# Gates without GpSimd and staging on both sides of SBUF, in an encoder layer with product-key experts

## The chip, the cores and the metric

The kernel runs on one core of one Trainium2 chip. The core has a matrix engine (PE), a vector engine (VectorE, DVE in the profile), a scalar engine (ScalarE, ACT), GpSimd (POOL), the sync engine's queue (SP) for transfers, and 16 DMA engines. Its on-chip memories are SBUF, with 128 partitions, and PSUM, where matrix products are summed. The metric is device time in microseconds for one execution. Before the change the median of three runs is 3086.2 us (3084.46 to 3092.26).

## The reference

One layer of an encoder over 1024 tokens of width 1024: a projection, differential attention and retention, an output projection added to x, and then PEER, a feed-forward layer made of 16384 single-neuron experts, of which each token uses 8 x 16. The change lies in PEER:

```python
q = (xb @ w_query).reshape(tb, PEER_HEADS, 2, PEER_KEY_DIM // 2)
s = jnp.einsum('thpd,hpnd->thpn', q, sub_keys)
top_s, top_i = lax.top_k(s, PEER_TOPK)                   # 16 of 128 rows, 16 of 128 columns
cand_s = top_s[:, :, 0, :, None] + top_s[:, :, 1, None, :]
cand_i = top_i[:, :, 0, :, None] * N_KEYS + top_i[:, :, 1, None, :]
best_s, pos = lax.top_k(cand_s, PEER_TOPK)               # the best 16 of the sums
eid = take_along_axis(cand_i, pos)
gate = softmax(best_s)
act = gelu(einsum('thkd,td->thk', expert_down[eid], xb))
out = einsum('thk,thkd->td', gate * act, expert_up[eid])
```

An expert is a pair (row, column) of a grid of 128 x 128.

## The kernel before

The eight blocks of 128 tokens are worked on in two ways after the output projection. Five of them (set B) compute PEER densely: the activations of all 16384 experts, times a gate that is zero for nearly all, times all expert values. The other three (set A) fetch the rows of their chosen experts one by one with indirect transfers that POOL issues (line 988) and that DVE reduces (lines 998 and 1007). Products in full precision are three products of parts: an operand is split by ACT into a high part (`uh`, `hh`, `vh`, `wqh`) and by DVE or POOL into the rest (`ul`, `hl`, `vl`, `wql`).

Four stretches follow one another:

- **The choice of experts** (648 to 899 us in the profile), for set B and one block of set A, so n = 6 blocks at once. For each of 8 heads and both key sets, PE computes queries (`pq`) and scores (`psc`), and DVE takes the best 16 (lines 723 to 728). Then `choose` finds where the winners came from: DVE compares positions with a ramp (line 778, `eq`, 6 x 16 x 16 elements in bf16), first for rows and then for columns, and POOL multiplies the result by the indices `tif` (line 779); sums over it give the expert's row and column. `sel` (line 788) takes the gate. POOL also makes `wql` (line 656), `pql` (636) and, for five blocks of experts whose dense activations are computed ahead here, `ul` (858).
- **The gates** (899 to 1124 us). For each of 5 blocks (i) the choices are transposed (`gtp`, copied to `kT` and `gT`). Then for each group of 4 tokens, 32 groups per block: DVE compares a ramp with the tokens' rows and columns at once (line 920, `oh`, bf16); ACT copies one half into `bo` in f32 (924); the other half is multiplied by the gate into `ao`, by POOL (927) in 29 groups of 32 and by ACT (930) in 3; PE multiplies the two for each token (933), which puts the gates of one token on the grid of experts in PSUM (`pg`, six buffers); and DVE (936, 13 groups of 32) or ACT (938, 19 of 32) copies them into `stg`, 64 KB per partition. When a block is done, eight transfers of 1 MB store `stg` to `g_dr` in DRAM (940), in runs of 512 bytes. `oh`, `bo` and `ao` have four buffers each, `stg` two, both in one pool.
- **The start of the dense stage** (1124 to 1222 us). Five blocks of expert weights, `first0` to `first4` (512 KB each), are loaded, split, and multiplied (`products`, `pa`, gelu into `hfirst`); beside each of them four of set A's fetched rows are reduced with `xng`. Then their gates are read back from `g_dr` into the same tiles, multiplied by `hfirst` (1070) and split again, and the product with the expert values begins (`up`, tiles `po`). `acc` holds the sums, begun with x.
- **The dense stage** (1222 us to the end): for the other blocks of experts the same, with the rest of the fetching beside it.

Instructions of one engine run in order. The program writes the work stage by stage; a scheduler orders each engine's queue by need, so operations of neighbouring steps mix. A tile pool on the left or right side of SBUF gives its room back when it closes, and what is placed there later waits until the last reader of the old tiles is done. The tiles of the fetched rows (`rows`, `xng`, `gacc`) and the `first` tiles lie on the right side.

## Time and profile before

| | us |
|---|---|
| median of three runs | 3086.2 |
| profiled execution, its own time | 3082.46 |
| its span, first to last instruction | 3080.7 |
| PE busy in the span | 2830.5 (92%) |
| DVE busy | 2556.9 (83%) |
| POOL busy | 1678.9 (54%) |
| ACT busy | 1055.1 (34%) |

The rows further down come from the trace of the profiled execution. A row of a timeline gives the start, the time, the engine, the line of the program, the operation and the tiles (out<-in), and in brackets the idle time before it with what ended it; equal operations in a row are one entry with a count. A row of a table by stretches gives, for PE, weight loads, DVE, ACT and POOL in this order, busy microseconds and the number of instructions, then the granted clock of PE as a share of full speed, the DMA engines' busy share and the rate in GB/s. Busy time includes time in which an operation has begun and stands still.

### The profile page before, as it was taken

The page shows a single profiled execution, that of the slowest core. Times are in us where ns is not written, and L with a number is a line of the kernel's source. Part 1 is how long each engine was busy: PE and PEld are TensorE (multiplying, and loading weights), DVE is VectorE, ACT ScalarE, POOL GpSimd, SP SyncE. Part 2 cuts the span into 40 slices and gives each one's busy share as a digit, 9 for nine tenths or more (in the row PEclk, how much of TensorE's full clock was granted, in tenths as well). Part 3 has the DMA queues.
Part 4 walks back from the last instruction along what each step waited for, and adds up shares of the span by engine and source line. Part 5 has one row for each costly group of instructions (what it writes and reads, how often), then busy time and mean ns, then how long its engine had stood idle before and what let it go on. Part 6 is the DMA issues. An engine that isn't in the chain of part 4 may idle for free.

```text
span 3080.7 us, 44740 instructions
## 1 busy us (share of the span) xinstructions
PE 2830.5 (92%) x15999; PEld 2512.8 (82%) x15999; DVE 2556.9 (83%) x4867; ACT 1055.1 (34%) x1734; POOL 1678.9 (54%) x1335
## 2 busy tenths in 40 slices
PE   8999798898978846999999999999999999999998
PEld 6887577698976646988888888898999889989997
DVE  6466587579999955899999998988999889889997
ACT  4444566422237742222322222222222222222222
POOL 3422455245659954566656556566554466565551
PEclk9999999999999977999999999999999999999999
DMA  4334865353205688998898888999999899999994
GB/s 166 108 118 142 194 123 110 133 195 129 104 18 138 190 224 318 326 324 319 302 323 292 305 328 332 328 331 322 338 324 326 295 355 327 327 333 332 331 323 157
DMA packets 334832, 770.87 MB, mean 250 GB/s; under 512 B 26640, under 2 KB 133776, under 8 KB 334608
## 3 DMA queue, kind: packets, MB, share of 16 engines
q0 software_dynamic: 128128, 438.36, 41.2%
q1 hardware_dynamic: 203888, 324.72, 31.8%
q10 hardware_dynamic: 2592, 4.93, 0.5%
q8 instruction: 126, 2.06, 0.3%
q14 instruction: 98, 0.80, 0.1%
HBM read 678.70 MB, written 89.19 MB: 249 GB/s over the span
## 4 chain that ended last, share of the span: by engine, by line
PE 19%; issue 17%; DVE 16%; POOL 10%; DMA 7%; ACT 2%; SPq 1%; POOLq 0%; DVEq 0%; ACTq 0%
POOL rows L988 8%; DVE rows L998 3%; PE po L73 3%; PE po L75 3%; DVE gacc L1007 3%; PE po L74 3%; PE pa L73 3%; PE pa L74 3%; PE pa L75 3%; DVE oh L920 2%; DMA ur<-ut 2%; DMA rows<-peer_u,idx 1%; DVE acc L1104 1%; DMA vr<-peer_v 1%; POOL ao L927 1%
## 5 line engine op out<-in xcount | busy, mean ns | idle before, releaser
L988 POOL DMA_INDIRECT rows<-peer_u,idx x384 | 525.8, 1369 | 411.3 <-DVE act L998 248.0
L73 PE MATMUL pa<-nThB,uh 128*128 128x320 f32 x2048 | 636.4, 311 | 54.7 <-ACT uh L1060 39.8
L988 POOL DMA_INDIRECT rows<-peer_v,idx x384 | 469.6, 1223 | 393.8 <-DVE gacc L1007 326.5
L75 PE MATMUL pa<-nThB,ul 128*128 128x320 f32 x2048 | 633.8, 310 | 14.1 <-DVE ul L1061 14.1
L74 PE MATMUL pa<-nTlB,uh 128*128 128x320 f32 x2048 | 634.3, 310 | 0.0
L73 PE MATMUL po<-vh,hh 128*128 128x512 f32 x1280 | 511.0, 400 | 46.0 <-DVE acc L1104 40.8
L75 PE MATMUL po<-vh,hl 128*128 128x512 f32 x1280 | 505.2, 395 | 0.0
L74 PE MATMUL po<-vl,hh 128*128 128x512 f32 x1280 | 504.3, 394 | 0.0
L1007 DVE SCALAR_TENSOR_TENSOR gacc<-rows,act,gacc 128x1024 f32<-128x1024 f32 x384 | 493.3, 1285 | 6.2 <-DMA rows<-peer_v,idx 5.3
L998 DVE CUSTOM_DVE_ANT_0 rows<-rows,xng 128x1024 f32<-128x1024 f32 x384 | 459.3, 1226 | 34.9 <-DMA rows<-peer_u,idx 20.5
L73 PEld LDWEIGHTS pa<-nThB,uh 128*128 128x128 f32 x2048 | 387.7, 189 | 61.0 <-ACT uh L1060 40.0
L75 PEld LDWEIGHTS pa<-nThB,ul 128*128 128x128 f32 x2048 | 387.8, 189 | 15.8 <-DVE ul L1061 15.4
L74 PEld LDWEIGHTS pa<-nTlB,uh 128*128 128x128 f32 x2048 | 387.6, 189 | 4.4
L73 PEld LDWEIGHTS po<-vh,hh 128*128 128x128 f32 x1280 | 244.0, 191 | 103.6 <-DVE acc L1104 49.6
L1092 ACT ACTIVATE vh<-vr 128x512 fp32r<-128x512 f32 x256 | 160.5, 628 | 414.4 <-DMA vr<-peer_v 197.2
L75 PEld LDWEIGHTS po<-vh,hl 128*128 128x128 f32 x1280 | 243.8, 190 | 54.8 <-DVE hl L1077 0.4
L74 PEld LDWEIGHTS po<-vl,hh 128*128 128x128 f32 x1280 | 244.1, 191 | 46.6
L1060 ACT ACTIVATE uh<-ur 128x1024 fp32r<-128x1024 f32 x118 | 125.2, 1061 | 360.5 <-PE pa L74 226.6
L1061 DVE TENSOR_TENSOR ul<-ur,uh 128x1024 fp32r<-128x1024 f32 x118 | 144.3, 1223 | 106.3 <-ACT uh L1060 104.6
L933 PE MATMUL pg<-ao,bo 128*128 128x128 f32 x1280 | 182.2, 290 | 40.3 <-POOL ao L927 31.7
L927 POOL TENSOR_TENSOR ao<-oh,gT 128x512 f32<-128x512 bf16 x145 | 206.9, 1461 | 22.0 <-DVE oh L920 22.0
L868 ACT ACTIVATE hf<-pa 128x320 f32<-128x320 f32 x246 | 105.7, 430 | 328.9 <-PE pa L75 319.0
(346 smaller groups left out, 5415.0 us busy)
## 6 DMA issues: line engine op xcount, KB each, us to landing
vr<-peer_v SPq DMA_DIRECT2D x256, 256.0 KB, 6.0
ur<-ut SPq DMA_DIRECT2D x123, 512.0 KB, 5.7
g_dr<-stg SPq DMA_DIRECT2D x40, 1024.0 KB, 10.1
gt<-g_dr SPq DMA_DIRECT2D x123, 320.0 KB, 4.9
wr<-w_in SPq DMA_DIRECT2D x48, 512.0 KB, 3.8
wqr<-wq SPq DMA_DIRECT2D x16, 576.0 KB, 5.3
wq_dr<-wqh SPq DMA_DIRECT2D x16, 576.0 KB, 4.7
wq_dr<-wql SPq DMA_DIRECT2D x16, 576.0 KB, 3.3
```

Of the source, the lines that this page charges most:

```text
L73: PE.matmul(out, ah, bh, start=first, stop=False)
L74: PE.matmul(out, ah, bl, start=False, stop=False)
L75: PE.matmul(out, al, bh, start=False, stop=last)
L868: S.activation(hf[:, cs], pa, AF.Gelu)
L927: G.tensor_tensor(ao, oh[0], bc(gT[:, q:q + 4, None], [P, 4, P]), op=ALU.mult)
L933: PE.matmul(pg[:, j], bo[:, j], ao[:, j], start=True, stop=True)
L988: G.indirect_dma_start(out=u, out_offset=None, in_=table, in_offset=bass.IndirectOffsetOnAxis(ap=idx, axis=0))
L998: V.tensor_tensor_reduce(out=u, in0=u, in1=xn, scale=1.0, scalar=0.0, op0=ALU.mult, op1=ALU.add, accum_out=act[:, k:k + 1])
L1007: V.scalar_tensor_tensor(o, v, act[:, k:k + 1], o, op0=ALU.mult, op1=ALU.add)
L1060: S.activation(uh, ur, AF.Copy)
L1061: V.tensor_tensor(ul, ur, uh.bitcast(F32), op=ALU.subtract)
L1092: S.activation(vh, vr, AF.Copy)
```

## The change

POOL's operations in the choice are issued in pieces: `wql` in three of 384 elements, the multiplication `eq` in three of 512, `ul` in two of 512. In the gates `ao` is always made by DVE and `stg` always copied by ACT. `stg` has one buffer on the left side of SBUF (blocks 0, 2, 4) and one on the right (blocks 1, 3). Once the stores of block 3 are written into the program, the right one is closed, and the tiles of fetched rows and the `first` tiles are placed there; the `first` loads go from ACT's queue, after the gates, to SP's, ahead of the last block's stores.

```diff
@@ -653,7 +653,9 @@
             wh = pool.tile([P, 9, P], F32R, name="wqh")
             wl = pool.tile([P, 9, P], F32R, name="wql")
             S.activation(wh, wr, AF.Copy)
-            G.tensor_tensor(wl, wr, wh.bitcast(F32), op=ALU.subtract)
+
+            for b in range(0, 9, 3):
+                G.tensor_tensor(wl[:, b:b + 3], wr[:, b:b + 3], wh[:, b:b + 3].bitcast(F32), op=ALU.subtract)
             for k, w in enumerate((wh, wl)):
                 nc.sync.dma_start(wq_dr[hp, k], w.bitcast(F32))
             return wh, wl
@@ -776,7 +778,10 @@
                 for a, pl in ((0, row), (1, col)):
                     eq = pw.tile(sh, BF16, name="eq")
                     V.tensor_tensor(eq, bc(pl[:, :, None, :], sh), bc(iot[:, None, :, :], sh), op=ALU.is_equal)
-                    (V if last and not a else G).tensor_tensor(eq, eq, bc(tif[:, :, a, :, None], sh), op=ALU.mult)
+                    en = V if last and not a else G
+                    for b in [(0, n)] if n < 4 else [(b, b + 2) for b in range(0, n, 2)]:
+                        o = eq[:, b[0]:b[1]]
+                        en.tensor_tensor(o, o, bc(tif[:, b[0]:b[1], a, :, None], [P, b[1] - b[0], TOPK, TOPK]), op=ALU.mult)
                     if wb > 1:
                         eqs.append((a, eq))
                     else:
@@ -855,7 +860,9 @@
             for b, e, ur in rooms:
                 (queue or nc.sync).dma_start(ur, ap["ut"][a][:, b:e])
                 S.activation(uh[:, b:e], ur, AF.Copy)
-                (en or V).tensor_tensor(ul[:, b:e], ur, uh[:, b:e].bitcast(F32), op=ALU.subtract)
+                for c in range(b, e, 4):
+                    (en or V).tensor_tensor(ul[:, c:c + 4], ur[:, c - b:c - b + 4], uh[:, c:c + 4].bitcast(F32),
+                                            op=ALU.subtract)
             return uh, ul
 
         def products(ps, hf, bufs, uh, ul):
@@ -899,10 +906,14 @@
 
 
         g_dr = dram.tile([P, P, wB], F32, name="g_dr")
+        pros = ExitStack()
         with ExitStack() as es:
             pc = es.enter_context(tc.tile_pool(name="gc", bufs=1))
             pw = es.enter_context(tc.tile_pool(name="gw", bufs=4))
-            pg_ = es.enter_context(tc.tile_pool(name="gs", bufs=2))
+
+            odd = ExitStack()
+            pgs = [es.enter_context(tc.tile_pool(name="gs0", bufs=1)),
+                   odd.enter_context(tc.tile_pool(name="gs1", bufs=1, side="right"))]
             ps = es.enter_context(tc.tile_pool(name="gps", bufs=2, space=PSUM))
             iop = pc.tile([P, P, 4], BF16, name="iop")
             G.iota(iop, pattern=[[1, P], [0, 4]], base=0, channel_multiplier=0, allow_small_or_imprecise_dtypes=True)
@@ -914,7 +925,7 @@
                 V.tensor_copy(kT, pT[:, 0:2])
                 gT = pw.tile([P, P], F32, name="gT", bufs=1)
                 V.tensor_copy(gT, pT[:, 2])
-                stg = pg_.tile([P, P, P], F32, name="stg")
+                stg = pgs[i % 2].tile([P, P, P], F32, name="stg")
                 for q in range(0, P, 4):
                     o2 = pw.tile([P, 2, P, 4], BF16, name="oh")
                     V.tensor_tensor(o2, bc(iop[:, None], [P, 2, P, 4]), bc(kT[:, :, None, q:q + 4], [P, 2, P, 4]),
@@ -923,25 +934,24 @@
                     bo = pw.tile([P, 4, P], F32, name="bo")
                     S.activation(bo, oh[1], AF.Copy)
                     ao = pw.tile([P, 4, P], F32, name="ao")
-                    if q // 4 % 11:
-                        G.tensor_tensor(ao, oh[0], bc(gT[:, q:q + 4, None], [P, 4, P]), op=ALU.mult)
-                    else:
-                        for j in range(4):
-                            S.activation(ao[:, j], oh[0][:, j], AF.Copy, scale=gT[:, q + j:q + j + 1])
+                    V.tensor_tensor(ao, oh[0], bc(gT[:, q:q + 4, None], [P, 4, P]), op=ALU.mult)
                     pg = ps.tile([P, 4, P], F32, name="pg", bufs=6)
...
                     dst, src = stg[:, :, q:q + 4], pg.rearrange("p t a -> p a t")
-                    if q // 4 % 5 in (0, 2):
-                        V.tensor_copy(dst, src)
-                    else:
-                        S.activation(dst, src, AF.Copy)
+                    S.activation(dst, src, AF.Copy)
                 for k in range(0, P, 16):
                     nc.sync.dma_start(g_dr.rearrange("a b t -> b a t")[:, k:k + 16, i * P:(i + 1) * P], stg[:, k:k + 16])
+                if i == (nB - 2 if nB % 2 else nB - 1):
+                    odd.close()
+                    gp = top.enter_context(tc.tile_pool(name="gp", bufs=1, side="right"))
+                    pp = pros.enter_context(tc.tile_pool(name="pro", bufs=1, side="right"))
+                    firsts = [pp.tile([P, DC * P], F32, name=f"first{a}") for a in range(FIRST)]
+                    for a, ur in enumerate(firsts):
+                        nc.sync.dma_start(ur.rearrange("p (c e) -> p c e", e=P), ap["ut"][a])
         early.close()
 
 
-        gp = top.enter_context(tc.tile_pool(name="gp", bufs=1, side="right"))
         late = {}
 
         def tail(t, o):
@@ -1119,30 +1129,27 @@
...
-            with tc.tile_pool(name="pro", bufs=1, side="right") as pp:
-                first = [pp.tile([P, DC * P], F32, name=f"first{a}") for a in range(FIRST)]
-                for a, ur in enumerate(first):
-                    S.dma_start(ur.rearrange("p (c e) -> p c e", e=P), ap["ut"][a])
-                load(FIRST)
...
+            load(FIRST)
+            for a, ur in enumerate(firsts):
+                raw[a] = ur.rearrange("p (c e) -> p c e", e=P)
...
+            for a in range(FIRST):
+                down(a)
+            pros.close()
```

**DVE, the beginning of the gates.** Before, `oh` is the comparison and `stg<-pg` the copy of a group out of PSUM:

```order
L914 CAST kT<-gtp 128x256
L916 COPY gT<-gtp 128x128
L920 TENSOR_TENSOR oh<-iop,kT 128x1024 x5
L936 COPY stg<-pg 128x128x4
L920 TENSOR_TENSOR oh<-iop,kT 128x1024 x2
L936 COPY stg<-pg 128x128x4
L920 TENSOR_TENSOR oh<-iop,kT 128x1024 x4
L936 COPY stg<-pg 128x128x4
```

and in the changed program, `ao<-oh,gT` is the multiplication by the gate:

```order
L925 CAST kT<-gtp 128x256
L927 COPY gT<-gtp 128x128
L931 TENSOR_TENSOR oh<-iop,kT 128x1024 x2
L937 TENSOR_TENSOR ao<-oh,gT 128x512 x2
L931 TENSOR_TENSOR oh<-iop,kT 128x1024 x2
L937 TENSOR_TENSOR ao<-oh,gT 128x512 x2
L931 TENSOR_TENSOR oh<-iop,kT 128x1024 x2
L937 TENSOR_TENSOR ao<-oh,gT 128x512 x2
```

The copies are gone from DVE, and each pair of comparisons is followed by its two multiplications.

**SP, the end of the gates.** `g_dr<-stg` are the stores of a block (32 for the first four), `x_dr` the residual x in DRAM, `gt` and the later `first` loads the gates read back. Before:

```order
L940 DMA g_dr<-stg 128x16x128 x32
L1044 DMA ur<-ut 128x1024
L940 DMA g_dr<-stg 128x16x128 x8
L1089 DMA vr<-peer_v 128x512 x2
L1143 DMA acc_10860<-x_dr_70 128x1024
L1143 DMA acc_10861<-x_dr_71 128x1024
L1143 DMA acc_10862<-x_dr_72 128x1024
L1143 DMA acc_10863<-x_dr_73 128x1024
L1143 DMA acc_10864<-x_dr_74 128x1024
L1053 DMA gt<-g_dr 128x640
L1004 DMA gacc<-x_dr_75 128x1024
L1141 DMA first_10868<-g_dr 128x640
```

and in the changed program:

```order
L944 DMA g_dr<-stg 128x16x128 x32
L951 DMA first_10471<-ut 128x1024
L951 DMA first_10472<-ut 128x1024
L951 DMA first_10473<-ut 128x1024
L951 DMA first_10474<-ut 128x1024
L951 DMA first_10475<-ut 128x1024
L1014 DMA gacc<-x_dr_75 128x1024
L1054 DMA ur<-ut 128x1024
L944 DMA g_dr<-stg 128x16x128 x8
L1099 DMA vr<-peer_v 128x512 x2
L1147 DMA first_10471<-g_dr 128x640
L1147 DMA first_10472<-g_dr 128x640
```

The five loads of weights stand between the fourth and the fifth block's stores, and the `acc` loads have gone behind the gates of the five blocks.

**ACT, the fifth block of the gates.** `xng` is the input that the first fetched rows are reduced with. Before:

```order
L924 ACTIVATE bo<-oh 128x512 x3
L938 ACTIVATE stg<-pg 128x128x4 x3
L1125 DMA first_10868<-ut 128x1024
L1125 DMA first_10869<-ut 128x1024
L1125 DMA first_10870<-ut 128x1024
L1125 DMA first_10871<-ut 128x1024
L1125 DMA first_10872<-ut 128x1024
L1060 ACTIVATE uh<-first_10868 128x1024
L994 DMA xng<-xn_dr_83 128x1024
L1060 ACTIVATE uh<-first_10869 128x1024
```

and in the changed program:

```order
L935 ACTIVATE bo<-oh 128x512
L942 ACTIVATE stg<-pg 128x128x4
L935 ACTIVATE bo<-oh 128x512
L1004 DMA xng<-xn_dr_83 128x1024
L942 ACTIVATE stg<-pg 128x128x4 x2
L935 ACTIVATE bo<-oh 128x512 x4
L942 ACTIVATE stg<-pg 128x128x4 x2
L935 ACTIVATE bo<-oh 128x512
L942 ACTIVATE stg<-pg 128x128x4
L935 ACTIVATE bo<-oh 128x512
```

The weight loads have left this queue; `bo` and `stg` alternate; and the load of `xng`, which stood behind all gates, stands ahead of the last eight `bo`.

## Rows read from the trace of the kernel before

**Rows 1.** Busy time by stage: stretch, length, busy us per engine, clock, DMA, GB/s:
```profile
648.50:899.00 250.50, 222.10 (x1549) 218.38 (x1547) 239.71 (x1327) 56.94 (x100) 143.68 (x93) 0.93 0.30 106
899.00:1124.10 225.10, 183.64 (x1292) 158.29 (x1290) 219.00 (x235) 167.29 (x315) 206.94 (x145) 0.98 0.55 152
1124.10:1222.00 97.90, 40.88 (x241) 39.89 (x241) 34.11 (x52) 11.78 (x20) 33.44 (x25) 0.71 0.96 324
1222.00:3080.70 1858.70, 1792.42 (x10000) 1620.36 (x10000) 1664.19 (x2654) 498.12 (x798) 1034.24 (x827) 0.99 0.89 316
```

**Rows 2.** One line's instructions (least/median/longest ns): the comparison of columns:
```profile
L778 DVE TENSOR_TENSOR eq<-col,iot x8: 951/3424/3426, 675.1 to 889.1; 128x1536 bf16<-128x1536 bf16 x8
```

**Rows 3.** Timelines of POOL and DVE in one head (start us, us):
```profile
828.85 2.78 POOL L779 TENSOR_TENSOR eq<-eq,tif 128x1536 bf16<-128x1536 bf16 x1 [6.13 <-DVE eq L778]
...
829.02 3.42 DVE L778 TENSOR_TENSOR eq<-col,iot 128x1536 bf16<-128x1536 bf16 x1
```

**Rows 4.** Timeline of DVE: small operations caught beside POOL:
```profile
672.56 2.46 DVE L765 TENSOR_TENSOR col<-tc__6080,ex 128x96 bf16<-128x96 f32 x1
...
678.60 2.84 DVE L788 TENSOR_TENSOR sel<-be,gsm 128x96 f32<-128x96 f32 x1
...
867.44 2.43 DVE L788 TENSOR_TENSOR sel<-be,gsm 128x96 f32<-128x96 f32 x1
```

**Rows 5.** One line's instructions: line 779 later, in pieces of 512:
```profile
L779 POOL TENSOR_TENSOR eq<-eq,tif x6: 1042/1060/2154, 1358.5 to 1483.5; 128x512 bf16<-128x512 bf16 x6
```

**Rows 6.** Busy time in three heads of the choice:
```profile
671.70:705.50 33.80, 33.05 (x258) 32.73 (x258) 31.84 (x156) 8.84 (x16) 25.14 (x16) 1.00 0.41 137
...
733.90:762.30 28.40, 25.11 (x176) 24.79 (x175) 28.26 (x166) 5.88 (x11) 18.10 (x12) 0.88 0.37 125
...
762.30:797.40 35.10, 32.16 (x231) 32.02 (x231) 30.80 (x165) 10.39 (x16) 20.68 (x13) 0.95 0.35 126
```

**Rows 7.** Timeline of DVE: the first instruction of the gates:
```profile
899.01 0.42 DVE L914 CAST kT<-gtp 128x256 bf16<-128x256 f32 x1 [3.07 <-PE gtp L912]
```

**Rows 8.** Timelines of DVE, POOL, ACT and PE in the gates:
```profile
944.37 1.88 DVE L920 TENSOR_TENSOR oh<-iop,kT 128x1024 bf16<-128x1024 bf16 x3
...
945.82 14.45 POOL L927 TENSOR_TENSOR ao<-oh,gT 128x512 f32<-128x512 bf16 x10 [1.70 <-DVE oh L920]
...
947.82 2.38 ACT L924 ACTIVATE bo<-oh 128x512 f32<-128x512 bf16 x4
...
948.63 4.12 PE L933 MATMUL pg<-ao,bo 128*128 128x128 f32 x32 [0.33 <-POOL ao L927]
...
953.03 1.16 PE L933 MATMUL pg<-ao,bo 128*128 128x128 f32 x8 [0.29 <-POOL ao L927]
```

**Rows 9.** One line's instructions: POOL's `ao`, and line 779 on DVE:
```profile
L927 POOL TENSOR_TENSOR ao<-oh,gT x145: 1032/1492/1512, 900.9 to 1121.2; 128x512 f32<-128x512 bf16 x145
...
L779 DVE TENSOR_TENSOR eq<-eq,tif x1: 1752/1752/1752, 887.4 to 887.4; 128x1536 bf16<-128x1536 bf16 x1
```

**Rows 10.** Timeline of DVE: a subtraction of 512 elements:
```profile
1213.38 0.69 DVE L1093 TENSOR_TENSOR vl<-vr,vh 128x512 fp32r<-128x512 f32 x1
```

**Rows 11.** Timelines of ACT, PE and POOL after the gates:
```profile
1123.53 0.60 ACT L938 ACTIVATE stg<-pg 128x512 f32<-128x512 f32 x1 [1.41 <-PE pg L933]
...
1163.26 0.64 PE L73 MATMUL pa<-nThB,uh 128*128 128x320 f32 x1 [39.77 <-ACT uh L1060]
...
1221.99 0.79 PE L73 MATMUL po<-vh,hh 128*128 128x512 f32 x1 [5.13 <-ACT hh L1076]
...
1160.27 0.94 POOL L988 DMA_INDIRECT rows<-peer_u,idx  x1 [0.30 <-issue]
...
1184.97 1.99 POOL L988 DMA_INDIRECT rows<-peer_u,idx  x1 [0.30 <-issue]
```

**Rows 12.** Chain of waits: the last stores landing (start us, us, what):
```profile
1145.49 10.85 DMA g_dr<-stg
```

**Rows 13.** Busy time in ten microseconds of loads without stores:
```profile
1160.00:1170.00 10.00, 6.74 (x30) 6.51 (x31) 2.45 (x2) 3.52 (x5) 4.11 (x4) 0.60 1.02 409
```

More of the change, by code (lines that the diff above doesn't have):

```diff
@@ L1119, in up @@
                         add(k, t)
-            with tc.tile_pool(name="pro", bufs=1, side="right") as pp:
-                first = [pp.tile([P, DC * P], F32, name=f"first{a}") for a in range(FIRST)]
-                for a, ur in enumerate(first):
-                    S.dma_start(ur.rearrange("p (c e) -> p c e", e=P), ap["ut"][a])
-                load(FIRST)
-                for a, ur in enumerate(first):
-                    raw[a] = ur.rearrange("p (c e) -> p c e", e=P)
-                    split_u(a)
-                    ready[a] = ready[a], pp.tile([P, wB], F32, name=f"hfirst{a}")
-                    products(ps, ready[a][1], 2, *ready[a][0])
-                    ready[a] = ready[a][1]
-                    for _ in range(4):
-                        next(gen)
-                split_u(FIRST)
-                load(FIRST + 1)
-                values(0)
-                values(1)
-                for a, ur in enumerate(first):
-                    gts[a] = ur[:, 0:wB]
-                    nc.sync.dma_start(gts[a], g_dr[a])
-                for t, o in zip(SETS["B"], acc):
-                    nc.sync.dma_start(o, x1_dr[t])
-                for a in range(FIRST):
-                    down(a)
+            load(FIRST)
+            for a, ur in enumerate(firsts):
+                raw[a] = ur.rearrange("p (c e) -> p c e", e=P)
+                split_u(a)
+                ready[a] = ready[a], pp.tile([P, wB], F32, name=f"hfirst{a}")
+                products(ps, ready[a][1], 2, *ready[a][0])
+                ready[a] = ready[a][1]
+                for _ in range(4):
+                    next(gen)
+            split_u(FIRST)
+            load(FIRST + 1)
+            values(0)
+            values(1)
+            for a, ur in enumerate(firsts):
+                gts[a] = ur[:, 0:wB]
+                nc.sync.dma_start(gts[a], g_dr[a])
+            for t, o in zip(SETS["B"], acc):
+                nc.sync.dma_start(o, x1_dr[t])
+            for a in range(FIRST):
+                down(a)
+            pros.close()
             for a in range(FIRST - 1, P):
```

## The prediction

> **What bounds the kernel now.** I read the busy time by stage first, then in each stage what the busiest engine waits for, and last the waits at the stage's end. The profiled execution took 3082.5 us for a span of 3080.7; the median of the runs shown is 3086.2, 3.7 us more, and every sum below is made on the profiled execution. The choice of experts takes 250.5 us with DVE busy for 239.7 of them; the gates 225.1 us with DVE busy for 219.0 and POOL for 206.9; then come 97.9 us in which PE works for 40.9 while the DMA engines are 0.96 busy; the long dense stage is PE's, 1792.4 of 1858.7 us [rows 1]. So the first two stages are set by DVE and POOL, the third by transfers, and the last, which the change hardly touches, by PE: what is gained before 1222 moves the end by as much.
>
> **POOL's operations in pieces.** In the choice a DVE operation that reads two operands from SBUF stands still while POOL computes. The comparison of columns takes 0.95 us where POOL is idle and 3.42 in seven of the eight heads [rows 2]: POOL's multiplication begins at 828.85, the comparison at 829.02, and it ends 0.8 us after POOL's 2.78 us are over [rows 3]. The eighth head multiplies its rows on DVE, so nothing is in the way. Smaller operations of 0.25 us are caught in the same way: one `col` of 2.46 us, and `sel` at 2.84 (twice) and 2.43 [rows 4]. All these stalls come to 7 x 2.47 + 2.2 + 2 x 2.6 + 2.2 = 26.9 us, the most that pieces can give.
>
> A piece of 512 elements takes POOL 1.04 us in the later, smaller choice [rows 5]. If DVE gets in after the piece under way, the comparison ends at about 828.85 + 1.04 + 0.95 = 830.85 instead of 832.4, so 1.6 us in each of seven heads, 11.2. The four small ones wait for one piece instead of a whole: about 1.2 + 3 x 1.8 = 6.6. POOL then works 3 x 1.04 = 3.1 us for 2.78, which its idle time hides, since it is busy for 143.7 of 250.5. Not all of it counts. In the first head shown (671.7 to 705.5, with the product of a block of experts in it) PE is busy for 33.05 of 33.8 us and DVE waits for PE; the head at 762.3 is alike; the others give PE 2 to 3 us of room in 28.4 [rows 6]. So I leave out the 4.6 and 3.4 us of those two heads and keep 17.8 - 8.0 = 9.8, say **10 us**, with 0 and 26.9 as ends. After the last head's exponential nothing more is won: the gelu and PE's last product queue behind it, and the first DVE instruction of the gates waits 3.07 us for the transposes behind that product [rows 7].
>
> The Trainium skill, "SBUF — State Buffer", section "SBUF: two separate sides", says that the port pair DVE shares with GpSimd is locked for a whole instruction and that the loser waits fully. The 3.42 us agree. It says nothing of who comes next when POOL has another piece queued; the gates below show the two alternating.
>
> **Gates without POOL.** A group of four tokens now costs 1.45 us: ten POOL operations in a row take 14.45 us, with DVE's `oh` between them. Three `oh` in a row take 1.88 us, one every 0.60; so 0.60 is DVE's part and 0.85 POOL's, since the two never run at once [rows 8]. Afterwards DVE makes `oh` and `ao` itself. `ao` on DVE is not in the trace. From the nearest rows: a subtraction of two SBUF operands of 512 elements takes 0.69 us by itself, about 0.60 in a row if it overlaps its neighbours as `oh` does; and the same kind of product as `ao`, bf16 with a repeated factor, ran once on DVE, 1536 elements in 1.75 us, 0.58 per 512 [rows 9, 10]. POOL's own least time for it, 1.03 [rows 9], is the upper end. I take 0.60, so 1.20 per group.
>
> The other engines: ACT does a `bo` and a `stg` copy per group; four `bo` take 2.38, one per 0.57 [rows 8], and a copy 0.60 [rows 11], so 1.17 when nothing makes it wait. PE needs 4.12 us for four groups, 1.03 each [rows 8]. But ACT alternates strictly in the new order, and a copy waits for the product of the `bo` before last: `bo` 0.67 (2.38 less three times 0.57), a product by itself 1.16 [rows 8], copy 0.60 make 2.43 per two groups, 1.22. I take 1.22: 160 x 1.22 = 195.2, plus 2.5 at start and end, 197.7 against 225.1: **27 us**. The copies taken from DVE (0.60 each, 13 of 32 groups) are in this, since DVE's whole row is counted anew.
>
> A wait is added here. ACT issues the load of `xng` before the last eight `bo` of the fifth tile. It goes where the fourth tile's staging was, so it waits for those stores, and the fifth tile's products stand behind it. Stores land 32.2 us after their tile's last copy: the last copy before ends at 1124.1, the last landing at 1156.3 [rows 11, 12]. ACT comes to the load 24 x 1.22 + 0.6 = 30 us into the fifth tile: it waits 2 us, so **25** remain.
>
> **The change to the dense stage.** Let T be the end of the last copy. Today the five first blocks of weights are loaded once the last stores have landed, T + 32; PE starts at T + 39, and its first product with `po` at 1222.0, T + 98 [rows 11]. Afterwards these loads wait only for the fourth tile's stores, which land at T - 7, so the five products (within the 40.9 us for which PE works in these 97.9) can start a few microseconds after T. That is not the gain, since `po` needs all gates back from DRAM, after the last stores, and DVE has twenty gathered rows to reduce first, in order. What is in the way is bytes: 97.9 us x 324 GB/s = 31.7 MB [rows 1]. The loads of `acc` (2.6 MB) now stand behind the gates, which leaves 29.1 MB, begun 7 us earlier. At 324 GB/s that ends at T + 83, and with 6 us for the last gates and the split at T + 89. But six of the 25 gathers (3.1 MB) only run ahead of what `po` needs, and reads alone go at 409 GB/s [rows 13]. With 32 us for the 8.4 MB of stores, as today, and 409 GB/s for the other 17.6 MB, 43 us, it is 75 us: T + 68, and `po` at T + 74. Between T + 74 and T + 89, nearer to the first since DVE takes the gathers one by one and cannot ask for more than six ahead, I take T + 76: **22 us**. Ends: T + 95, where stores come last of all, and T + 60, where stores and reads fill each other's gaps and all 26 MB go at 409 GB/s (64 us, begun 7 us before T, and 3 for the split of the first block).
>
> POOL issues a gather in 0.94 us when DVE is idle and in 1.99 when it is not [rows 11]; the six early ones fall into the fifth tile, where DVE never pauses, and then take 6 x 2.3 = 14 us instead of 7.5. They lie beside the loads, so I cost this at nothing. The same page of the Trainium skill ("SBUF — State Buffer", section "SBUF: two separate sides") warns that GpSimd cannot write descriptors while DVE holds the pair. Taken strictly, the gathers would only start at T and `po` would come up to 7 us later; the 1.99 us in the trace say slowed, not stopped.
>
> **Sum:** 10 + 25 + 22 = 57 us. 3082.5 - 57 = 3025.5, and 3.7 more for the median: **3029 us**.
>
> **Rivals.** (a) Pieces give nothing: POOL keeps its turn between its own pieces, or PE takes over in every head. For it: PE is busy for 222 of 250 us of the stage. Against: the alternation in the gates. 3039 us. (b) The last stores come late: each shares the engines with gathers, whose rows of 4 KB are eight times as long as a store's runs of 512 bytes. Then `po` is at T + 89 to T + 95, the third gain 3 to 9 us: 3042 to 3048. The Trainium skill, "DMA: Bandwidth & Descriptors", section "Queues, rings and completion order", says that an engine takes turns between queues packet by packet, which favours (b); no row here shows such stores beside gathers. (c) The opposite, both at full rate side by side: `po` at T + 60, 16 us better: 3013. (d) In the gates the loop of `bo`, product and copy runs at 1.35 us a group, with a wait of 0.07 at each hand-over: 160 x 1.35 + 2.5 = 218.5, a gain of 7 instead of 27: 3049. (e) Slower: `ao` on DVE reads every fourth element and repeats the gate, and costs what POOL's costs. With the other terms kept (10 + 22 - 2 = 30 us), slower by over 9.3 us begins where the gates last 225.1 + 39.3 = 264 us; that is 160 x (0.60 + x) + 2.5, so x = 1.03 us, POOL's least. At POOL's median of 1.49 us they would last 337, and the kernel 3168. Against: the row of 1.75 us.
>
> **Numbers.** My forecast 0.58 (its own range 3014 to 3043), (a) 0.12, (b) 0.11, (c) 0.07, (d) 0.08, (e) 0.04. (a) and (b) together, or (a) and (d), reach 3058; (c) with all 26.9 us of stalls gone 2996. I take 2996 to 3058. About 0.3%, 9 us, is what a measurement of this kernel can tell from no change: faster 0.93, same 0.03, slower 0.04.
>
> **What would show it.** In the profile after: the comparison of columns at 1.8 us; the span from the first `kT` to the last `stg` copy near 198 us with DVE busy throughout and `ao` at 0.6 to 0.7; PE's first product of the dense stage 3 to 8 us after that copy; the first `po` near 76 us after it. I am wrong if `ao` takes over 0.8, if ACT waits more than 5 us for `xng`'s place, or if the gates come back from DRAM so late that `po` stays at 90 us or more.

## The result and the profile after

The changed kernel took 3036.2 us (median of 4 runs, 3029.1 to 3038.6) beside 3085.3 for the kernel before (4 runs): ratio 0.9835, 95% interval [0.9817, 0.9853], 49 us less. The forecast was 3029 with a range of 2996 to 3058. The profiled execution took 3035.0 us with a span of 3033.2.

Busy time by stage of the kernel after, with the columns of [rows 1]: the choice, the gates, the start of the dense stage up to the first `po`, and the rest.

```profile
646.50:896.61 250.11, 221.32 (x1547) 217.90 (x1546) 229.27 (x1330) 56.82 (x100) 158.79 (x154) 0.92 0.30 106
896.61:1100.75 204.14, 184.35 (x1292) 159.35 (x1289) 198.10 (x334) 182.42 (x321) 7.64 (x7) 0.97 0.67 192
1100.75:1164.70 63.95, 37.66 (x240) 36.87 (x241) 33.58 (x50) 12.86 (x20) 24.02 (x17) 0.81 1.03 359
1164.70:3033.20 1868.50, 1795.13 (x10002) 1622.32 (x10000) 1664.02 (x2652) 497.74 (x797) 1035.30 (x828) 0.98 0.89 316
```

Against [rows 1]: the choice is as long as before (250.1 for 250.5), though DVE is busy for 10 us less; the gates take 204.1 for 225.1; the way to the first `po` 64.0 for 97.9; and the rest is 9.8 us longer. So the 47.5 us between the spans are 0.4 + 21.0 + 33.9 - 9.8, plus 2.0 by which the choice began earlier. The forecast had 10 + 25 + 22, 57 us up to `po`, and 55.3 came. That this sum fits is luck: two terms were too large, by 9.6 and 4.0, and one too small, by 11.9. The medians fell by 49, which is 8 less than forecast.

**The choice.** The comparison of columns, one line's instructions (least/median/longest ns), against [rows 2]:

```profile
L780 DVE TENSOR_TENSOR eq<-col,iot x8: 957/1694/1696, 672.0 to 886.1; 128x1536 bf16<-128x1536 bf16 x8
```

It fell from 3.42 to 1.69 us, as forecast. But a head that was 28.35 us from one row comparison to the next (735.90 to 764.25) is 28.42 now. The reason stands 16 us further on. POOL and DVE there, in the kernel before:

```profile
751.50 2.68 POOL L656 TENSOR_TENSOR wql<-wqr,wqh 128x1152 fp32r<-128x1152 f32 x1
...
754.97 0.60 DVE L772 TENSOR_TENSOR eq<-eq 128x768 bf16<-128x768 bf16 x1
755.69 0.33 DVE L772 TENSOR_TENSOR eq<-eq 128x384 bf16<-128x384 bf16 x1
756.22 0.23 DVE L772 TENSOR_TENSOR eq<-eq 128x192 bf16<-128x192 bf16 x1
756.38 0.24 DVE L734 TENSOR_TENSOR cs<-tv 128x96 f32<-128x96 f32 x1
```

And in the same head of the kernel after:

```profile
751.50 3.39 POOL L658 TENSOR_TENSOR wql<-wqr,wqh 128x384 fp32r<-128x384 f32 x3
...
752.33 0.60 DVE L774 TENSOR_TENSOR eq<-eq 128x768 bf16<-128x768 bf16 x1
753.06 0.96 DVE L774 TENSOR_TENSOR eq<-eq 128x384 bf16<-128x384 bf16 x1
754.22 0.79 DVE L774 TENSOR_TENSOR eq<-eq 128x192 bf16<-128x192 bf16 x1
754.92 1.06 DVE L736 TENSOR_TENSOR cs<-tv 128x96 f32<-128x96 f32 x1
```

Before, the long stall had put DVE behind POOL: its sums of pairs began 19.1 us into the head, 0.8 after POOL's subtraction was over. Now DVE comes 1.9 us sooner (17.1), POOL is 0.7 later (16.3 to 19.7 us), and the sums meet the subtraction: 0.63 + 0.56 + 0.82 = 2.0 us of new stalls for the 1.73 saved.

The other heads bear this out. The first five, which have such a second subtraction of weights, became 0.1 to 1.1 us longer. The sixth and the seventh, which have none, became 1.3 us (28.29 to 26.99) and 3.1 us (30.28 to 27.20) shorter.

**The gates.** Groups by line, shapes apart (busy us, mean ns | idle before):

```profile
L935 ACT ACTIVATE bo<-oh 128x512 f32<-128x512 bf16 x160 | 107.3, 673 | 1.9 <-DVE oh L931 1.9
L937 DVE TENSOR_TENSOR ao<-oh,gT 128x512 f32<-128x512 bf16 x160 | 104.3, 699 | 3.2 <-PE pg L940 2.2 <-issue 1.0
L931 DVE TENSOR_TENSOR oh<-iop,kT 128x1024 bf16<-128x1024 bf16 x160 | 104.0, 698 | 1.8 <-ACT bo L935 1.8
L942 ACT ACTIVATE stg<-pg 128x512 f32<-128x512 f32 x160 | 95.4, 598 | 20.5 <-PE pg L940 10.0 <-issue 5.5
```

DVE's two instructions take 0.70 us each with overlap, 1.20 a group, as estimated. The wait for `xng`, on ACT's timeline:

```profile
1082.29 0.68 ACT L935 ACTIVATE bo<-oh 128x512 f32<-128x512 bf16 x1
1086.90 0.36 ACTq L1004 DMA_DIRECT2D xng<-xn_dr  x1
1087.31 1.09 ACT L942 ACTIVATE stg<-pg 128x512 f32<-128x512 f32 x2 [4.34 <-issue]
```

The fourth tile's last copy ended at 1055.41 and its stores landed 31.5 us later (32.2 forecast), but ACT was at the load after 27.6 us and not 30.

**The start of the dense stage.** SP's transfers, ACT and PE (an idle time and its releaser in brackets):

```profile
1100.78 48.97 SPq L944 DMA_DIRECT2D g_dr<-stg  x8
1149.79 4.56 SPq L1099 DMA_DIRECT2D vr<-peer_v  x2
1154.45 2.60 SPq L1147 DMA_DIRECT2D first<-g_dr  x5
1157.16 0.63 ACT L1102 ACTIVATE vh<-vr 128x512 fp32r<-128x512 f32 x1 [29.00 <-DMA vr<-peer_v]
...
1159.53 0.64 PE L73 MATMUL pa<-nThB,uh 128*128 128x320 f32 x1 [24.08 <-ACT hfirst L875]
...
1164.70 0.40 PE L73 MATMUL po<-vh,hh 128*128 128x512 f32 x1
```

PE's first product of the stage came 1.0 us after the last copy (3 to 8 forecast). The stores stand on SP for 49 us and the first gates are asked for at 1154.45, T + 54 (T is the end of the last copy); before, the last store had landed at T + 32 [rows 12]. Still `po` comes at T + 64 and not at T + 98. The whole way from T - 7 to `po`, as one stretch:

```profile
1093.75:1164.70 70.95, 43.48 (x284) 42.20 (x284) 38.17 (x58) 18.06 (x30) 27.24 (x20) 0.82 1.03 364
```

### The profile page after: what moved, and what is told of

It reads as the page before. It is cut to its first block, busy times and chain, and to the rows that moved or that the text cites. A ratio compares the mean times of both kernels' runs of the same rounds, so it can differ in the third digit from the quotient of the medians.

```text
span 3033.2 us, 44587 instructions
## 1 busy us (share of the span) xinstructions
PE 2827.2 (93%) x15999; PEld 2510.9 (83%) x15999; DVE 2524.9 (83%) x4964; ACT 1071.3 (35%) x1739; POOL 1487.9 (49%) x1257
## 4 chain that ended last, share of the span: by engine, by line
PE 20%; issue 17%; DVE 14%; POOL 9%; DMA 6%; SPq 2%; ACT 2%; POOLq 0%; DVEq 0%; ACTq 0%
POOL rows L998 8%; PE po L73 3%; DVE gacc L1017 3%; PE po L75 3%; PE po L74 3%; DVE rows L1008 3%; PE pa L73 3%; PE pa L74 3%; PE pa L75 3%; SPq L944 2%; DMA ur<-ut 2%; PE pg L940 2%; DMA vr<-peer_v 1%; DMA rows<-peer_u,idx 1%; DVE acc L1114 1%
## 5 line engine op out<-in xcount | busy, mean ns | idle before, releaser
L1103 DVE TENSOR_TENSOR vl<-vr,vh 128x512 fp32r<-128x512 f32 x256 | 177.8, 695 | 45.6 <-ACT vh L1102 45.5
L1114 DVE TENSOR_TENSOR acc<-po,acc 128x512 f32<-128x512 f32 x320 | 205.0, 687 | 4.1 <-PE po L75 4.1
```

What stands on the lines that cost most here:

```text
L1103: V.tensor_tensor(vl, vr, vh.bitcast(F32), op=ALU.subtract)
L1114: V.tensor_tensor(acc[t][:, ks], pos[t], acc[t][:, ks], op=ALU.add)
```

## Experiments

All times by stage are from one profiled execution of each kernel; T is the last copy to `stg`, "choice" runs from the first row comparison to the first `kT`, "gates" from there to T. Ratios are against runs of the kernel before that were taken beside each version (median 3085 us for the changed kernel, 3088 to 3092 for the others; the profiled execution of 3082.5 lies under that). e4 and e8 were run once, and only their choice is read.

```
                       choice  at   length  gates  T..po  po..end  ratio  [95%]
before                       671.7  227.3   225.1   97.9  1858.7
after                        669.7  226.9   204.1   64.0  1868.5   0.9835 [0.9817, 0.9853]
e1  pieces only              674.8  226.4   225.1   96.4  1868.6   0.9995 [0.9982, 1.0008]
e2  gates only               678.2  227.7   197.9   96.5  1869.6   0.9902 [0.9887, 0.9918]
e3  staging only             670.7  229.2   225.2   65.1  1872.9   0.9913 [0.9895, 0.9931]
e4  no multiplication        676.7  216.1
e5  xng by GpSimd            674.0  227.9   197.9   70.5  1861.2   0.9827 [0.9812, 0.9841]
e6  vr by ACT                672.7  226.6   204.6   66.4  1864.8   0.9826 [0.9801, 0.9850]
e7  gathers later            675.3  226.5   202.8   42.3  1893.5   0.9839 [0.9825, 0.9853]
e8  six pieces               669.5  232.3   204.2   64.7  1867.9
e9  merged comparison        672.5  228.0   204.7   63.8  1871.7   0.9835 [0.9815, 0.9855]
e10 e5 + e7 + rate           670.1  227.5   197.9   49.8  1884.2   0.9821 [0.9798, 0.9843]
e11 e9 + e10                 675.1  229.3   197.8   48.8  1887.3   0.9822 [0.9799, 0.9845]
e12 e11, sel by ACT          678.1  224.5   197.9   49.9  1878.0   0.9800 [0.9787, 0.9813]
```

**One part alone.** e1, e2 and e3 are the kernel before with one part of the change each: the three loops that cut GpSimd's operations; `ao` on DVE and all copies on ACT; `stg` on two sides and the first blocks' loads behind the fourth tile.

```diff
-            G.tensor_tensor(wl, wr, wh.bitcast(F32), op=ALU.subtract)
+            for b in range(0, 9, 3):
+                G.tensor_tensor(wl[:, b:b + 3], wr[:, b:b + 3], wh[:, b:b + 3].bitcast(F32), op=ALU.subtract)
...
```

> The kernel before with GpSimd's operations in pieces and nothing else. Prediction's term: the column comparison falls from 3.42 to 1.7 us in seven heads and the first kT starts 10 us earlier; time 3075. What the profile after suggests instead (stalls go, but two heads are PE's and new stalls of about 1 us hit small DVE operations that were clear before): first kT only 2 to 3 us earlier, time 3082 to 3083, ratio 0.999. If pieces were worth the 10 us and something else in the changed kernel hid it, the ratio is 0.997 or less.

```diff
-                    if q // 4 % 11:
-                        G.tensor_tensor(ao, oh[0], bc(gT[:, q:q + 4, None], [P, 4, P]), op=ALU.mult)
...
+                    V.tensor_tensor(ao, oh[0], bc(gT[:, q:q + 4, None], [P, 4, P]), op=ALU.mult)
...
```

> The kernel before with the gates made without GpSimd (ao on DVE, all copies to stg on ACT) and nothing else. If the gate loop is the 1.20 us a group that the profile after shows and xng's wait is what kept it at 204 us, kT to the last stg copy is 199 us here (225.1 before) and the rest keeps its length: time 3085 - 26 = 3059. If ACT's hand-over limits the loop apart from that wait, the stage is 204 us again and the time 3064.

```diff
-            pg_ = es.enter_context(tc.tile_pool(name="gs", bufs=2))
+            pgs = [es.enter_context(tc.tile_pool(name="gs0", bufs=1)),
+                   odd.enter_context(tc.tile_pool(name="gs1", bufs=1, side="right"))]
...
```

> The kernel before with the two-sided staging and the early loads of the first blocks and nothing else; GpSimd keeps its part of the gates, so its gathers stand behind its last ao. Prediction's term: last stg copy to first po 76 us instead of 98, time 3085 - 22 = 3063. As the profile after shows it (64 us): 34 us less, 3051, of which the dense stage gives some 10 back: 3061. If the early gathers are what made the 64 us, it is 70 us or more here, since no gather can start before the gates end.

The pieces are worth 0.9 us of choice, and nothing that can be measured in the time. The gates without `xng`'s wait take 197.87 us, the 197.7 of the forecast. The staging alone brings `po` to T + 65. Its first gather is issued only 1.7 us before T (1125.05), so the early gathers are not the reason:

```profile
1123.38 1.10 POOL L998 DMA_INDIRECT rows<-peer_u,idx  x1 [0.17 <-issue]
```

e3 moves the loads of `acc` behind the gates as well, and does not tell their part from that of the early loads. The three ratios less one sum to -0.0190 and the whole change has -0.0165, a difference within the intervals. In the profiles the way from the first `kT` to `po` is 28.6 us shorter in e2, 32.7 in e3 and 54.9 in the changed kernel, 6.4 less than the sum. That is the size of `xng`'s wait, which e2 does not have, but e5 below takes the wait away and `po` comes no sooner.

e1 and e2 also answer the 9.8 us by which the dense stage grew: they contain the old dense stage instruction for instruction, and it took 1868.6 and 1869.6 us there. The 1858.7 of [rows 1] was a short one, and the choice, whose lead-up hardly changed, began anywhere from 669.5 to 678.2. Two profiles compared over the long stage can be 10 us apart for nothing. That none of the 9.8 us belongs to the change is not shown: e3 won 30.8 us from the choice's start to `po`, and its ratio gives 21 to 32.

**What the pieces could give.** e4 leaves GpSimd's multiplication in the first choice out, so that other experts come out; e8 makes it in six pieces.

```diff
-                    (V if last and not a else G).tensor_tensor(eq, eq, bc(tif[:, :, a, :, None], sh), op=ALU.mult)
+                    if n < 4 or last and not a:
+                        (V if last and not a else G).tensor_tensor(eq, eq, bc(tif[:, :, a, :, None], sh), op=ALU.mult)
```

> The kernel before with GpSimd's multiplication in the first choice of experts left out (so other experts come out, and only the choice is read from this run, not the time). By the prediction all stalls that it causes, 26.9 us, go, 8 of them in heads that PE sets: the first kT starts some 19 us earlier than 899.0. If the choice is set by PE and by DVE's waits for it, it starts less than 6 us earlier, and DVE's waits for PE's scores grow by what the stalls lose.

```diff
-                    for b in [(0, n)] if n < 4 else [(b, b + 2) for b in range(0, n, 2)]:
+                    for b in [(0, n)] if n < 4 else [(b, b + 1) for b in range(n)]:
```

> The changed kernel with GpSimd's multiplication in six pieces of 256 elements. By the prediction's reasoning a DVE operation waits for one piece only, so the column comparison falls from 1.70 to about 1.4 us and the choice (first row comparison to first kT, 226.9 us) gets 1 to 3 us shorter. If the lock is only dealt out differently (each further piece catches a further DVE operation), more small operations take 0.5 us or more, and the choice is as long as before or longer, 227 to 230 us, since six pieces keep GpSimd busy longer.

Two heads of e4 by busy time, the first with a block's product in it, the second without:

```profile
676.73:712.20 35.47, 35.47 (x276) 35.47 (x275) 31.60 (x166) 9.98 (x18) 19.75 (x14) 1.00 0.37 131
712.20:738.25 26.05, 25.84 (x202) 25.52 (x200) 25.91 (x166) 5.53 (x12) 13.67 (x10) 1.00 0.40 138
```

The first is PE's (busy all of 35.47 us), as the prediction left it out; the second fell from 28.4 to 26.05, and the choice as a whole is 11.2 us shorter than before (216.1 for 227.3), of which three pieces won 0.4 to 0.9. So both theories in e4's expectation missed: the stalls that the multiplication causes are on the path, but are 11 us and not 19. Six pieces cut the comparison to 1.26 us and made the choice 5.4 us longer, with the small operations of a head caught one after another. What catches them there is again the second subtraction (724.02 to 727.39) and the POOL work behind it:

```profile
725.57 0.96 DVE L774 TENSOR_TENSOR eq<-eq 128x384 bf16<-128x384 bf16 x1
726.72 0.78 DVE L774 TENSOR_TENSOR eq<-eq 128x192 bf16<-128x192 bf16 x1
727.43 1.06 DVE L736 TENSOR_TENSOR cs<-tv 128x96 f32<-128x96 f32 x1
728.41 1.06 DVE L775 TENSOR_TENSOR sel<-eq 128x96 f32<-128x96 bf16 x1
```

So pieces deal the stalls out differently; e8 speaks against the step that counted only the caught operation.

**The wait on ACT and the way through DRAM.**

> The changed kernel with the load of xng issued by GpSimd, which is idle in the gates, and not by ACT. If ACT's wait for the room of xng is what makes the gates 204.1 us where the gates alone took 197.9, kT to the last stg copy is 198 us here, and the time 6 us under the changed kernel: 3030, ratio 0.982. If the early loads and gathers slow the loop by themselves (transfers and GpSimd's descriptors beside DVE), the stage stays at 202 us or more and nothing is won.

```diff
-                (nc.sync if i else S).dma_start(xn, xn_dr[t])
+                (nc.sync if i else G).dma_start(xn, xn_dr[t])
```

> The changed kernel with the first two loads of vr issued by ACT, so that they don't stand behind the last stores on SP. If PE's idle time from 1135 to 1159 is ACT standing at vh (29 us for vr) with two gelus behind it, PE goes on with the fifth and sixth products at about T + 36, and po comes when the first gates are there, at T + 59 to 61 instead of T + 64; the time is 3 to 6 us lower, 3031 to 3033. If the gates' way through DRAM is all that counts, po stays at T + 63 to 65 and nothing is won.

```diff
-                nc.sync.dma_start(vr, ap["peer_v"][a * P:(a + 1) * P, 512 * k:512 * k + 512])
+                (nc.sync if n > 1 else S).dma_start(vr, ap["peer_v"][a * P:(a + 1) * P, 512 * k:512 * k + 512])
```

e5 is the instructive one. The wait went and the gates fell to 197.9, and `po` did not come earlier: from the first `kT` to `po` it is 268.3 us, 268.1 in the changed kernel. The 6.3 us were turned into waiting for transfers (T + 70.5 for T + 64.0): the stores now stand on SP for 55.8 us and not for 49.0.

```profile
1099.84 55.80 SPq L944 DMA_DIRECT2D g_dr<-stg  x8
```

The transfers could not start sooner, since their room comes free with the fourth tile's stores: the load of `xng` is issued 190.3 us after the first `kT` in the changed kernel and 191.4 in e5. And without ACT's wait DVE has no pause, so that the first gather stands on POOL until DVE's row of `oh` and `ao` is over:

```profile
1094.40 3.88 POOL L998 DMA_INDIRECT rows<-peer_u,idx  x1 [0.37 <-DVE ao L937]
...
1094.86 1.29 DVE L931 TENSOR_TENSOR oh<-iop,kT 128x1024 bf16<-128x1024 bf16 x2
1096.07 1.29 DVE L937 TENSOR_TENSOR ao<-oh,gT 128x512 f32<-128x512 bf16 x2
```

It is done 0.92 us after DVE's last `ao`, and in e10, e11 and e12 (3.88, 4.44 and 4.38 us) it is the same within 0.01. The ratio, 0.9827, cannot be told from 0.9835. In e6 `vr` was issued at 1103.5, and `vh` still waited 29 us:

```profile
1162.37 1.15 ACT L1102 ACTIVATE vh<-vr 128x512 fp32r<-128x512 f32 x2 [29.04 <-DMA g_dr<-stg]
```

The releaser has changed its name: `vr` was asked for 59 us before `vh` began, and what ended the wait was the stores. So the theory that `vr` stands behind the stores on SP's queue fell. The likely reason is that `vh` lies where `stg` was, but this is not shown: no run put `vh` elsewhere, and whether that would let PE go on is open.

> The changed kernel with the twenty gathers between the first products moved behind them (none is left out). If the last stores take 50 us because they share the DMA engines with the gathers, they are landed 32 to 36 us after T as before the change, and po comes at T + 42 to 46, some 20 us earlier; the end gains that, if the later stage has room for twenty more gathers on DVE and in the transfers (3016), and nothing or less where it has not (3036 or more). If the stores are slow for another reason, po stays at T + 60 or later.

```diff
-                for _ in range(4):
+                for _ in range(0):
                     next(gen)
```

SP's stores in e7, and the DMA share and rate (last two columns) of the stretch in which they stand on the queue:

```profile
1104.64 29.00 SPq L944 DMA_DIRECT2D g_dr<-stg  x8
```

```profile
1104.61:1133.60 28.99, 24.04 (x155) 24.07 (x156) 4.81 (x4) 6.87 (x10) 0.00 (x0) 0.88 1.06 329
```

The same stretch of the changed kernel:

```profile
1100.75:1149.80 49.05, 32.48 (x216) 31.70 (x216) 27.36 (x41) 7.80 (x12) 24.02 (x17) 0.89 1.06 379
```

29 us for 49, and `po` at T + 42: the gathers are what makes the stores slow, on DMA engines that are full either way. The Trainium skill, "DMA: Bandwidth & Descriptors", section "Queues, rings and completion order", says that an engine takes turns between queues, and these two rows agree. The end is where it was: the left-over gathers ran past PE, whose last `po` product began at 3011.0, 29.4 us before the end (12.0 in the changed kernel). The chain of waits (start us, us, what) ends in them:

```profile
3004.96 5.20 DMA rows<-peer_v,idx
3010.20 1.27 DVE gacc L1017
...
3023.02 1.30 DVE gacc L1017
```

> The changed kernel with the twenty gathers behind the first products, xng loaded by GpSimd, and the later gathers' rate raised from 6.0 to 6.2 per block, which asks for the twenty within the rest. If the run without early gathers lost its 22 us only at the end, where the left-over gathers finished 30 us before the end and after PE's products, then the gates take 198 us, po comes at T + 42, and the end follows PE: some 20 us under the changed kernel, 3016, ratio 0.977. If the later stage is as full as it can be (DVE at 0.9), PE waits for DVE there by about 1.2 us for each gather moved, 25 us, and the time stays at 3033 to 3040.

```diff
-RATE = 6.0
-EVERY = 6
+RATE = 6.2
+EVERY = 6.2
...
```

The rest of this edit is that of e5 and e7. With the higher rate the last gather is issued at 2964 and added up by 2990, well before PE's last product (3018), and `po` to the end is 1884.2 us, 15.7 more than in the changed kernel, for 20.4 won before it (first `kT` to `po` 247.7 for 268.1). PE's idle time after `po` grew by 6.2 us and its busy time by 9.5; from one profile the second cannot be told from the spread of unchanged stages. The ratio, 0.9821, shows no gain over 0.9835. Of the two theories the second holds in its time (3032.9 us), but not in its reason: PE did not wait 25 us more.

**Clearing the first stall.** e9 takes the pieces out and makes both comparisons one instruction, e11 adds e10, and e12 also gives the product behind it to ACT:

> The changed kernel with GpSimd's operations whole again, and in the first choice both comparisons made by one DVE instruction of 3072 elements, so that GpSimd's multiplications start when no two-operand DVE instruction is near. If the lock costs only where such an instruction meets it, the five heads set by DVE take 26.0 us as without the multiplication, the choice (row comparison to first kT) falls from 226.9 to about 216 us, and the time to 3025, ratio 0.979. If the multiplications then only catch other operations, as the pieces did, the choice stays at 226 us or more and the ratio at 0.983.

```diff
+                    eq2 = pw.tile(both, BF16, name="eq", bufs=2)
+                    V.tensor_tensor(eq2, bc(rc[:, :, None, :], both), bc(iot[:, None, :, :], both), op=ALU.is_equal)
...
```

> The two together: merged comparison, whole GpSimd operations, twenty gathers behind the first products, xng by GpSimd, rate 6.2. If both terms hold and add, 11 and 20 us under the changed kernel: 3005, ratio 0.973. If only the choice's term holds, 3025.

> The run of the two together with one more step: the product of the exponentials and the reciprocal sums (sel, the DVE instruction that took 2.85 us right behind the merged comparison) made by ACT, in six instructions a head. If the lock costs only where a two-operand DVE instruction meets GpSimd, nothing is near the first multiplication now: heads set by DVE take 26.0 to 27.2 us (28.3 to 29.5 in the two runs with the merged comparison), the choice from row comparison to first kT 216 to 221 us instead of 228 to 229, and the time is 8 to 12 us under the run of the two together: 3028, ratio 0.9795. If the stall again finds the next small operation (sums of pairs, pair scores), the heads stay at 28 us or more and the choice at 226 us or more.

```diff
-                V.tensor_tensor(g3, be, bc(sm[:, :, None], [P, n, TOPK]), op=ALU.mult)
+                    for t in range(n):
+                        S.activation(g3[:, t], be[:, t], AF.Copy, scale=sm[:, t:t + 1])
...
```

The comparison was free of stalls (1.76 us for both), and in e9 the next two-operand instruction stood for the multiplication's whole length:

```profile
738.15 2.78 POOL L786 TENSOR_TENSOR eq<-eq,tif 128x1536 bf16<-128x1536 bf16 x1 [8.14 <-DVE eq L779]
...
738.20 2.85 DVE L795 TENSOR_TENSOR sel<-be,gsm 128x96 f32<-128x96 f32 x1
```

So e9's choice stayed at 228.0 us and its ratio at 0.9835, and e11, for which 3005 or 3025 us were expected, took 3038.9 (0.9822): neither of its terms came. In e12 the stall of `sel` is gone, and in the heads with a second subtraction of weights the sums of pairs are caught by it:

```profile
729.25 2.66 POOL L656 TENSOR_TENSOR wql<-wqr,wqh 128x1152 fp32r<-128x1152 f32 x1
...
729.71 2.62 DVE L772 TENSOR_TENSOR eq<-eq 128x768 bf16<-128x768 bf16 x1
```

Those heads take 28.9 to 29.0 us; the two without that subtraction take 26.15 and 27.17, near e4's floor of 26.0. Both theories were half right: a stall arises only where instructions meet, and after each repair they met again. The choice is 224.5 us. e12 has the lowest median, 3030.1 us, ratio 0.9800 [0.9787, 0.9813], though it is not clear of e10 and e11. Its interval lies just under that of the changed kernel, 11 us by the two ratios. Its profile has 2.4 us less in the choice, 20.3 less from `kT` to `po`, and 9.5 more after `po`; how much of the last is spread is not settled by one profile each. Moving the second subtraction away from the sums was not tried.

## Why the prediction was right, and which steps failed

- **Gates: right.** 160 groups at 1.22 us and 2.5 us gave 197.7; alone they take 197.87 (e2), so 27.2 us against 27. Rivals (d) and (e) are out: 0.70 us for `ao`.
- **`xng`'s wait: too small.** 2 us forecast; the gates of e5, without it, are 6.3 us shorter. ACT stood for 4.3, being 2.4 us sooner at the load than forecast. The other 2.0 lie behind the load, where DVE and ACT wait for PE and for each other four times more before the stage ends; the step did not count them. It cost nothing in the end, since transfers set `po` anyway. "More than 5 us of waiting" was the mark for being wrong; the wait by itself stayed under it, its cost did not.
- **Pieces: wrong.** 10 us forecast, 0.4 to 0.9 measured. The comparison did fall to 1.7 us. The failed step is "DVE gets in after the piece under way", summed over operations as if each stall removed were time: it followed DVE to the end of the caught operation and not to its next meetings with POOL. e8, e9 and e12 show the stall moving on each time. Rival (a) had the right size with another reason. The row of `sel` beside POOL in e9 agrees with the Trainium skill, "SBUF — State Buffer", section "SBUF: two separate sides" (the loser waits for the whole instruction): 2.85 us beside a multiplication of 2.78.
- **Start of the dense stage: bytes right, overlap wrong.** T + 76 forecast, T + 64 measured, so 34 us and not 22. The term that failed is "32 us for the stores and 409 GB/s for the rest" in a row. Stores and gathers ran together: from T - 7 to `po` 70.95 us went at 364 GB/s, 25.8 MB, which is the prediction's own 26 MB. So the bytes were right, and their going one kind after the other was wrong. That is nearly rival (c), which had 409 GB/s and T + 60, and half of rival (b) as well: the stores came late (49 us, 29 without gathers) and the gates were asked for last, but the other bytes had moved meanwhile. The six early gathers were costed at nothing, and in the changed kernel that was so: they took 0.95 to 1.10 us each from 1088.11 on, beside a DVE that ACT's wait had left with pauses. The reason given, "slowed, not stopped", does not hold in general: without those pauses the first gather stood for 3.88 us (e5).
- **The rest.** The dense stage was costed at no change. The 9.8 us by which it was longer lie within the spread of unchanged code (1858.7 to 1869.6 us in the kernel before, e1 and e2); whether a few of them belong to the change stays open.

Up to `po` the profiles show 0.4 + 21.0 + 33.9 = 55.3 us; by the ratio the change is worth 45 to 56. The terms up to `po` are read from one profile each, and e1, e2 and e3 give the same sizes apart (0.9, 27.2 without the wait, 32.7).

## What to carry to other kernels

When two engines make each other wait, a stall removed only counts if the faster engine does not run into the next operation of the slower one: follow both timelines for a whole period of the loop, not to the end of the operation that was caught. Where a stage is set by bytes in flight, a wait taken away from an engine can come back as a wait for transfers, as 6.3 us did in e5, so compare the whole way from one fixed event to another (first `kT` to first `po`), not the stage that was edited. And before explaining 10 us in an unchanged stage of 1860, look at it in two kernels that contain it unchanged.

## What the runs showed of the hardware

- Stores of 8.4 MB in runs of 512 bytes stood on their queue for 29 us without gathers, at 329 GB/s in all, and for 49 us beside gathers of 4 KB rows, at 379 GB/s (e7 and the changed kernel): mixing delayed the stores and raised the rate.
- The issue of a gather on POOL, 0.95 us beside an idle DVE, took 3.88 to 4.44 us when DVE ran two-operand instructions without a pause (e5, e10, e11, e12), and ended 0.92 to 0.93 us after the last of them. A gather of the changed kernel took 0.98 us although two `oh` ran for most of that time (1089.51), so what decides is open.
- Cutting a multiplication of 1536 elements into three made POOL's two per head 6.80 us long from first to last, against 6.45 before (736.94 to 743.39), of which 0.89 was a wait for DVE.
- The program up to the choice, nearly the same in all kernels, took 669.5 to 678.2 us.
